# Leaving the first shift out of the normalised rows of a hybrid attention layer, and adding its product where each projection leaves its bank

## The chip, the cores and the metric

One Trainium2 chip, one of its cores. The metric is device time in microseconds (us) of one execution of the whole kernel. The engines are named PE (TensorE), ACT (ScalarE), DVE (VectorE), POOL (GpSimd) and SP (SyncE, which here only issues DMAs).

## The reference, cut to what matters

One layer of an encoder runs over two request groups with the same weights: 1024 prompt tokens, and 32 sample tokens that see a cache of 512. D_MODEL is 1024. Each group has one vector `c`, from which the modulation vectors come. The part that the change touches is the way into the one combined projection:

```python
ada = jax.nn.silu(c) @ w_ada + b_ada                 # w_ada: 1024 x 6144
sh1, sc1, gt1, sh2, sc2, gt2 = [a[:, None, :] for a in jnp.split(ada, 6, axis=-1)]
h = rms_norm(x, g_pre_mix) * (1 + sc1) + sh1
p = h @ w_in                                         # w_in: 1024 x 4256
q_lat, c_kv, k_r, q_b, k_b, v_b, g_a, g_b = jnp.split(p, IN_SPLITS, axis=-1)
```

The eight parts of `p` feed two attention branches: latent attention (`q_lat`, `c_kv`, `k_r`) and stick-breaking attention (`q_b`, `k_b`, `v_b`, eight heads of 64), which are merged by the sigmoids of `g_a` and `g_b`. An output projection and a convolutional feed-forward part (1024 to 5632, and 2816 back to 1024) follow. All is float32. Outputs are the two groups' rows and the new cache entries, among them the K and V rows of the stick-breaking branch.

## The kernel before, in words

Everything is kept transposed: features on the 128 partitions, tokens along the free axis. The 1024 prompt tokens and the 32 sample tokens stand side by side, T = 1056 columns. A float32 product is made of three products of shorter numbers: each operand is split into a high part (`hi`, on ACT) and the remainder (`lo`, on DVE), and `mm3` multiplies high by high, high by low and low by high into one PSUM bank.

`stage_h` makes the normalised, modulated rows. Eight tiles of x (`load`) are fetched and scaled by their root mean square. `ada_half` makes shift and scale for one half of the 1024 features: eight DMAs of 512 KB of `w_ada`, 32 small products, two transposes (line 239), one addition of the bias. `norm_T` transposes x on PE (line 263), applies scale and shift with one ACT instruction per 512 columns (line 265), and DVE splits the result into `Hht` and `Hlt` (lines 268 and 269), eight tiles of 128 features each. The order written down is: first half of the modulation, rows of tokens 0 to 511 and 512 to 1023 for those features, then two weight tiles, then the second half of the modulation and the rows for it.

`w_in_tile` fetches 128 columns of `w_in` and splits them; there are 34 such tiles. `mtile` makes the product of one weight tile with the rows in three blocks of NB = 352 columns (`BLK`), 8 x 3 = 24 PE instructions a block, each block in one PSUM bank. There are eight banks: two tagged `mm`, two `tr`, three `s`, one `pv`.

`stage_sb` runs over four pairs of heads. `sb_pair` makes Q (split as it leaves the bank, scaled by 0.125), K and V, puts K and V into natural order by transposes for the cache outputs (`to_natural`), and sweeps the blocks of queries (`attend`: scores at lines 452 to 456, `sb_weights` on ACT and DVE, transposes, values). After each pair `gates` makes four of the 16 gate tiles; DVE copies each block out of its bank (line 633) and a DMA stores it. Between them `ada_step` makes the other four modulation vectors. `stage_lat` makes the rotated key, the two kv-latent tiles and the three query-latent tiles; a query-latent block is read from its bank by ACT twice (high part, line 60; square, line 809) and by DVE once (line 810). Merge, MLA attention, feed-forward and output stages follow; they don't use the rows `Hht` and `Hlt`.

The order of instructions on each engine isn't that of the source: a planner orders them when the program is built, by its own costs and the data they wait for, so that gate products stand between the steps of the attention. Each engine then works its list in order. Buffers rotate in the order of the source: a pool gives a tag so many buffers, and a new tile waits for the last reader of the tile that had its buffer.

Of the kernel before, what the change touches and what calls it, by code (L numbers as in the profile page):

```python
# [39 lines left out]
class K:  # L40
# [183 lines left out]
    def ada_half(self, hf, wp, tp):  # L224

        nc, a = self.nc, self.a
        acc = self.tl(tp, [P, 256], F32, f"ada{hf}")
        ps = self.bank("s")
        for k in range(KT):
            w = self.tl(wp, [P, 2, 512], F32, "wr")  # L230
            nc.sync.dma_start(w, a["w_ada"][0, k * P : (k + 1) * P].rearrange("p (v h n) -> p v h n", v=6, h=2)[:, 0:2, hf])
            for j in range(4):
                c = (j % 2) * 256
                nc.tensor.matmul(ps[32 * j : 32 * j + 32, :256], self.cT[:, k], w[:, j // 2, c : c + 256],
                                 start=k == 0, stop=k == KT - 1)
        nc.vector.tensor_copy(acc, ps[:, :256])
        tr = self.bank("s")
        for c in range(2):
            nc.tensor.transpose(tr[:, c * P : c * P + P], acc[:, c * P : c * P + P], self.idt)
        for c in range(2):  # L240
            k = slice(4 * hf + c, 4 * hf + 4, 2)
            nc.vector.tensor_tensor(self.adaT[:, 0:2, k],
                                    tr[:, c * P : c * P + P].rearrange("p (v j r) -> p v j r", v=2, j=2)[:, :, :, 0:2],
                                    self.bT[:, :, k].unsqueeze(3).broadcast_to([P, 2, 2, 2]), ALU.add)
        self.gain(self.g1, 1, 0, 4 * hf, 4)


    def norm_T(self, t0, xs, g, sv, tp, k0=0, k1=KT):


        nc = self.nc
        if t0 < 8:
            n = len(xs) * P
            m = 512 // n
            c = slice(t0 * P, t0 * P + n)
            for k in range(k0, k1, m):
                tr = self.bank("tr")
                f = self.tl(tp, [P, 512], F32, "hf").rearrange("p (k c) -> p k c", k=m)
                for e in range(m):
                    kc = slice((k + e) * P, (k + e) * P + P)  # L260
                    for j, x in enumerate(xs):
                        o = e * n + j * P
                        nc.tensor.transpose(tr[:, o : o + P], x[:, kc], self.idt)
                for e in range(m):
                    nc.scalar.activation(f[:, e], tr[:, e * n : e * n + n], AF.Identity,
                                         bias=self.adaT[:, sv, k + e, 0:1], scale=g[:, k + e, 0:1])
                h, l = self.Hht[:, k : k + m, c], self.Hlt[:, k : k + m, c]
                nc.vector.tensor_copy(h, f)
                nc.vector.tensor_tensor(l, f, h.bitcast(F32), ALU.subtract)
        else:  # L270
            tr = self.bank("tr")
            for c in range(2):
                nc.tensor.transpose(tr[:, c * P : c * P + P], xs[0][:, c * P : c * P + P], self.idt)
            f = self.tl(tp, [P, 512], F32, "hf")[:, :256].rearrange("p (k t) -> p k t", t=TS)
            for k in range(k0, k1):
                j, c = k // 2, k % 2
                nc.scalar.activation(f[:, k], tr[:, c * P + 32 * j : c * P + 32 * j + 32],
                                     AF.Identity, bias=self.adaT[:, sv, k, 1:2], scale=g[:, k, 1:2])
            f, h, l = (x[:, k0:k1] for x in (f, self.Hht[:, :, TP:T], self.Hlt[:, :, TP:T]))
            nc.vector.tensor_copy(h, f)  # L280
            self.lo(l, f, h)
# [22 lines left out]
    def new_H(self):  # L304
        self.Hp = self.tc.alloc_tile_pool(name=self.nm("H"), bufs=1, side="right", reuse_waits="tile")
        self.Hht = self.Hp.tile([P, KT, T], F32R, name=self.nm("hh"))
        self.Hlt = self.Hp.tile([P, KT, T], F32R, name=self.nm("hl"))
        self.Hh = [self.Hht[:, k] for k in range(KT)]
        self.Hl = [self.Hlt[:, k] for k in range(KT)]

    def stage_h(self):
# [3 lines left out]
        with self.tc.tile_pool(name="st_h", bufs=2, reuse_waits="tile") as tp, self.tc.tile_pool(name="wada", bufs=8, reuse_waits="tile") as wp:  # L315
# [9 lines left out]
            def norm(t, hf):  # L325
                self.norm_T(t, xts[t : t + 4] if t < 8 else [xs], self.g1, 0, tp, 4 * hf, 4 * hf + 4)
# [8 lines left out]
            for t in range(4, 8):  # L335
                load(t)
            norm(4, 0)
            xs = self.tl(tp, [P, 256], F32, "xs")
            self.quarters(xs, a["x_sample"][0])
            w = [self.w_in_tile(672), self.w_in_tile(672 + 512)]  # L340
            self.in_w = w
            self.ada_half(1, wp, tp)
            nc.vector.tensor_scalar(xs, xs, self.rstd_s(xs, tp), None, ALU.mult)
            norm(0, 1)
            norm(8, 0)
            norm(4, 1)
            norm(8, 1)
# [14 lines left out]
    def w_in_tile(self, c0):  # L362
# [3 lines left out]
        h, l = self.wsplit(raw)  # L366
        v = lambda t: t.rearrange("p (k c) -> p k c", k=8)
        return v(h), v(l)
# [13 lines left out]
    def sb_pair(self, p):  # L382
# [5 lines left out]
        wh, wl = self.w_in_tile(q0)  # L388
        for c0, n, ps in self.mtile(wh, wl, self.Hh, self.Hl, self.BLK, KT):
            m = min(n, TP - c0)  # L390
            c = slice(c0, c0 + m)
            self.hi(Qe[0:64, c], ps[0:64, :m], 0.125)
            self.hi(Qo[64:128, c], ps[64:128, :m], 0.125)
            st = nc.vector.scalar_tensor_tensor
            st(Qe[64:128, c], ps[0:64, :m], 0.125, Qe[0:64, c].bitcast(F32), ALU.mult, ALU.subtract)
            st(Qo[0:64, c], ps[64:128, :m], 0.125, Qo[64:128, c].bitcast(F32), ALU.mult, ALU.subtract)
            if m < n:
                nc.scalar.mul(self.qsb[:, p], ps[:, m:n], 0.125)
# [5 lines left out]
        wh, wl = self.w_in_tile(k0)  # L404
        for c0, n, ps in self.mtile(wh, wl, self.Hh, self.Hl, self.BLK, KT, "mm" if p else "s"):
            nc.scalar.copy(kf[:, c0 : c0 + n], ps[:, :n])
# [27 lines left out]
        wh, wl = self.w_in_tile(v0)  # L434
        for c0, n, ps in self.mtile(wh, wl, self.Hh, self.Hl, self.BLK, KT):
            nc.scalar.copy(vf[:, c0 : c0 + n], ps[:, :n])  # L436
# [188 lines left out]
    def gates(self, ms):  # L625
        nc = self.nc
        for m in ms:
            wh, wl = self.w_in_tile(2208 + m * P)
            if self.ada_todo:
                self.ada_step(2, self.W, self.At)  # L630
            for c0, n, ps in self.mtile(wh, wl, self.Hh, self.Hl, self.BLK, KT):
                g = self.tl(self.At, [P, 512], F32, "nat")
                nc.vector.tensor_copy(g[:, :n], ps[:, :n])
                nc.gpsimd.dma_start(self.gd[m, :, c0 : c0 + n], g[:, :n])

    def att_pools(self):
# [13 lines left out]
        nc.sync.dma_start(self.qt, self.a["k_ropeq"])  # L650
# [58 lines left out]
    def stage_lat(self):  # L709
# [15 lines left out]
        def latent(m0, n, pool, tag):  # L725
            f = []
            for m in range(m0, m0 + n):
                x = self.tl(pool, [P, T], F32, tag)
                f.append(x)
                wh, wl = self.w_in_tile(m * P)  # L730
                for c0, n_, ps in self.mtile(wh, wl, self.Hh, self.Hl, self.BLK, KT, "mm s s"):
                    nc.scalar.copy(x[:, c0 : c0 + n_], ps[:, :n_])
# [33 lines left out]
        for c0, n, ps in self.mtile(hv, lv, self.Hh, self.Hl, self.BLK, KT, "mm s s"):  # L766
# [4 lines left out]
            nc.vector.tensor_tensor(ta[64:128, :n], ps[0:64, :n], ct[0:64, :n], ALU.mult)  # L771
            nc.vector.tensor_tensor(tb[64:128, :n], ps[64:128, :n], ct[64:128, :n], ALU.mult)
# [28 lines left out]
        sq = self.tl(self.At, [P, BIG], F32, "big")  # L801
        for m in range(3):
            wh, wl = self.w_in_tile(m * P)
            g = self.gvT[:, 16 + m : 17 + m]
            for c0, n, ps in self.mtile(wh, wl, self.Hh, self.Hl, self.BLK, KT, "mm s s"):
                c, ps = slice(c0, c0 + n), ps[:, :n]
                self.hi(self.QLh[m][:, c], ps, g)
                d = self.tl(self.At, [P, 512], F32, "nat")[:, :n] if m else sq[:, c]
                nc.scalar.activation(d, ps, AF.Square)
                nc.vector.scalar_tensor_tensor(self.QLl[m][:, c], ps, g, self.QLh[m][:, c].bitcast(F32), ALU.mult, ALU.subtract)  # L810
# [973 lines left out]
```

## Time and profile before

| | |
|---|---|
| median of 3 runs | 1828.43 us (1828.35 to 1831.26) |
| the profiled execution | 1828.67 us |
| its span, first to last instruction | 1826.9 us |
| granted PE clock, mean | 0.987 |
| DMA over the span | 124 GB/s |

In the views below, a row of busy time by stretch reads: stretch in us, its length, then for PE, PE's weight loads (PEld), DVE, ACT and POOL the busy us and the number of instructions, the granted clock, the share of the 16 DMA engines' time, and GB/s. A row for one tile or line shows the engines that touch it. A row of the timeline reads: start in us, duration in us, engine, line, operation, output and inputs with partitions and elements, count, and in brackets the idle time before it and what ended it. A row of the waits reads: who waited for whom, us in total, times, longest. Matmuls are pipelined, so their starts tell the pace and their durations overlap.

### The profile page before, as it was taken

How to read it: one execution, taken by the hardware profiler on the slowest of the kernel's cores; microseconds unless marked ns; L12 is line 12 of the kernel's file. 1: busy time of each engine (PE TensorE's matmuls, PEld its weight loads, DVE VectorE, ACT ScalarE, POOL GpSimd, SP SyncE). 2: the span in 40 equal slices, each digit the busy share in tenths (PEclk: the TensorE clock that was granted, in tenths of full speed). 3: DMA queues.
4: the chain of work that ended last, by engine and by line, in shares of the span. 5: the costliest groups of instructions: out<-in, count | busy, mean ns of one | idle time of the engine just before them, and what ended most of it. 6: DMA issues, size and time to landing. Idle time of an engine off the chain costs nothing. (4 is left out here: it accounts for less than half of the span.)

```text
span 1826.9 us, 30116 instructions
## 1 busy us (share of the span) xinstructions
PE 1745.1 (96%) x11610; PEld 1552.6 (85%) x11610; DVE 1263.8 (69%) x2099; ACT 1001.0 (55%) x1913; POOL 257.4 (14%) x522
## 2 busy tenths in 40 slices
PE   6999999999899999999989998999999999999997
PEld 3888878878778988888878877999999999977876
DVE  4677377486378457777666677987877777788546
ACT  4565366564366458788687256544544444544432
POOL 2112111111111101111110022221211111110001
PEclk8999999999999999999999999999999999999999
DMA  9223333233232112222238352244233333497536
GB/s 339 74 88 111 94 99 87 76 99 101 93 97 82 54 57 72 80 71 77 64 123 269 124 179 108 67 152 140 93 122 132 101 111 132 166 338 257 164 90 220
DMA packets 182319, 228.61 MB, mean 125 GB/s; under 512 B 13509, under 2 KB 130208, under 8 KB 182176
## 3 DMA queue, kind: packets, MB, share of 16 engines
q1 hardware_dynamic: 166752, 182.93, 31.7%
q0 software_dynamic: 15424, 43.76, 6.8%
q8 instruction: 91, 1.49, 0.3%
q14 instruction: 52, 0.43, 0.1%
HBM read 174.86 MB, written 51.79 MB: 124 GB/s over the span
## 5 line engine op out<-in xcount | busy, mean ns | idle before, releaser
L60 ACT ACTIVATE wh<-wr 128x1024 fp32r<-128x1024 f32 (+6 forms) x187 | 150.7, 816 | 264.8 <-PE s L1248 86.6
L63 DVE TENSOR_TENSOR wl<-wr,wh 128x1024 fp32r<-128x1024 f32 (+6 forms) x187 | 169.5, 913 | 135.7 <-ACT wh L60 133.9
L67 PE MATMUL mm<-hh,wh 128*128 128x352 f32 x696 | 229.9, 330 | 0.6 <-ACT big L436 0.6
L69 PE MATMUL mm<-hh,wl 128*128 128x352 f32 x696 | 228.9, 329 | 0.0
L68 PE MATMUL mm<-hl,wh 128*128 128x352 f32 x696 | 228.0, 328 | 0.0
L67 PEld LDWEIGHTS mm<-hh,wh 128*128 128x128 f32 x696 | 132.1, 190 | 6.5 <-DVE ada L201 2.5
L69 PEld LDWEIGHTS mm<-hh,wl 128*128 128x128 f32 x696 | 132.1, 190 | 1.1 <-issue 0.8
L68 PEld LDWEIGHTS mm<-hl,wh 128*128 128x128 f32 x696 | 131.9, 189 | 1.3 <-issue 0.4
L530 PE MATMUL tr<-c,A 128*128 128x128 f32 x576 | 93.8, 277 | 5.4 <-ACT A L478 4.2
L1249 PE MATMUL s<-T,wl 128*128 128x256 f32 (+1 forms) x328 | 93.4, 285 | 0.0
L1248 PE MATMUL s<-T,wh 128*128 128x256 f32 (+1 forms) x328 | 93.3, 285 | 0.0
L1247 PE MATMUL s<-T,wh 128*128 128x256 f32 (+1 forms) x328 | 93.3, 284 | 0.0
L474 DVE TENSOR_TENSOR_SCAN A<-A 128x128 f32<-128x128 f32 (+8 forms) x66 | 87.8, 1343 | 0.3
L1385 DVE SCALAR_TENSOR_TENSOR u<-u,c,u 128x1058 f32<-128x1058 f32 x68 | 86.9, 1315 | 1.2
L530 PEld LDWEIGHTS tr<-c,A 128*128 128x128 f32 x576 | 66.6, 140 | 15.9 <-ACT A L478 10.2
L63 DVE TENSOR_TENSOR PTl<-tr,PTh 128x512 fp32r<-128x512 f32 x96 | 62.9, 683 | 24.1 <-ACT PTh L60 23.5
L1247 PE MATMUL tr<-T,wh 128*128 128x272 f32 (+1 forms) x272 | 77.9, 286 | 0.0
L1249 PE MATMUL tr<-T,wl 128*128 128x272 f32 (+1 forms) x272 | 77.4, 285 | 0.0
L1248 PE MATMUL tr<-T,wh 128*128 128x272 f32 (+1 forms) x272 | 77.3, 284 | 0.0
L478 ACT ACTIVATE A<-A 128x128 f32<-128x128 f32 (+8 forms) x66 | 44.3, 680 | 60.0 <-DVE A L477 59.7
L63 DVE TENSOR_TENSOR wl<-S,wh 128x1024 fp32r<-128x1024 f32 x40 | 48.9, 1222 | 37.5 <-ACT wh L60 37.5
L1247 PE MATMUL mm<-T,wh 128*128 128x256 f32 (+1 forms) x256 | 73.2, 286 | 0.0
(598 smaller groups left out, 5571.8 us busy)
## 6 DMA issues: line engine op xcount, KB each, us to landing
wr<-in_w_ada_dram SPq DMA_DIRECT2D x48, 512.0 KB, 5.0
wr<-in_w_up_dram SPq DMA_DIRECT2D x44, 512.0 KB, 4.1
dr<-in_w_down_dram SPq DMA_DIRECT2D x43, 512.0 KB, 5.8
wr<-gdn SPq DMA_DIRECT2D x34, 512.0 KB, 4.5
wr<-in_w_in_dram SPq DMA_DIRECT2D x33, 512.0 KB, 4.0
gdn<-u POOLq DMA_DIRECT2D x23, 512.0 KB, 4.5
gd<-nat POOLq DMA_DIRECT2D x48, 176.0 KB, 2.5
t<-gd SPq DMA_DIRECT2D x16, 528.0 KB, 4.7
```

Source lines behind the costliest of these rows:

```text
L60: self.nc.scalar.activation(out, in_, AF.Identity, scale=scale)
L63: return self.nc.vector.tensor_tensor(out, full, hi.bitcast(F32), ALU.subtract)
L67: m(ps, lh, rh, start=start, stop=False)
L68: m(ps, lh, rl, start=False, stop=False)
L69: m(ps, ll, rh, start=False, stop=stop)
L474: nc.vector.tensor_tensor_scan(r, r, r, 0.0, ALU.add, ALU.bypass)
L478: nc.scalar.activation(A[:, :w], A[:, :w], AF.Exp)
L530: nc.tensor.transpose(tr[:, (2 * s + q) * P : (2 * s + q + 1) * P], at[q][:, b * P : b * P + P], self.idt)
L1247: m(ps[:, :n], w[0][:, k], x[0][:, k, c], start=first and k == 0, stop=False, skip_group_check=True)
L1248: m(ps[:, :n], w[0][:, k], x[1][:, k, c], start=False, stop=False, skip_group_check=True)
L1249: m(ps[:, :n], w[1][:, k], x[0][:, k, c], start=False, stop=k == 3, skip_group_check=True)
L1385: nc.vector.scalar_tensor_tensor(y, u[:, w : w + YW], self.cvT[:, w, cc : cc + 1], y, ALU.mult, ALU.add)
```

## The change

`ada_half` becomes `ada_first`, which makes one whole vector: the scale first, the shift last. The rows of the prompt get the scale alone; the transposed bank is split directly, high part by ACT, remainder by DVE. `Hht` and `Hlt` get two more columns (T to T + 2) that both hold the prompt's shift. The sample's rows still get a shift: the difference of the two groups' shifts, so that the prompt's shift is what is missing from all columns.

For each weight tile the block with columns 704 to 1057 (`SHB`, 354 columns) is now made first; its column 352 is the product of the shift with the weight tile. It is copied out (`bias`), and every block is added to it as it leaves its bank: by ACT's `plus`, in the gates by DVE. Only in the first head pair the blocks 0 and 1 of Q and K come first, in four banks, and the third blocks after them. The 0.125 of Q goes into its weight tile. In the query latents each sum is first written to a tile `nat`, from which high part, remainder and square are made. The table `qt` for the queries is loaded in `stage_lat`, no more in `att_pools`.

```diff
-    def ada_half(self, hf, wp, tp):
+    def ada_first(self, v, wp, tp):
...
-            nc.sync.dma_start(w, a["w_ada"][0, k * P : (k + 1) * P].rearrange("p (v h n) -> p v h n", v=6, h=2)[:, 0:2, hf])
+            nc.sync.dma_start(w, a["w_ada"][0, k * P : (k + 1) * P, v * D : v * D + D])
...
     norm_T:
-                    nc.scalar.activation(f[:, e], tr[:, e * n : e * n + n], AF.Identity,
-                                         bias=self.adaT[:, sv, k + e, 0:1], scale=g[:, k + e, 0:1])
-                nc.vector.tensor_copy(h, f)
-                nc.vector.tensor_tensor(l, f, h.bitcast(F32), ALU.subtract)
+                self.hi(h, tr, gk)
+                nc.vector.scalar_tensor_tensor(l, tr, gk, h.bitcast(F32), ALU.mult, ALU.subtract)
...
     stage_h, after load(0) to load(3):
-            self.ada_half(0, wp, tp)
-            norm(0, 0)
+            self.ada_first(1, wp, tp)
+            self.gain(self.g1, 1, 0)
+            w = [self.w_in_tile(672, 0.125)]
...
             for t in range(4, 8):
                 load(t)
-            norm(4, 0)
+            self.norm_T(0, xts[:4], tp, ("tr", "tr", "s", "s", "s"))
+            w.append(self.w_in_tile(672 + 512))
...
-            self.ada_half(1, wp, tp)
+            self.norm_T(4, xts[4:], tp, ("tr",))
...
+            self.ada_first(0, wp, tp)
+            h, l = (x[:, :, T : T + 2] for x in (self.Hht, self.Hlt))
+            sh = self.adaT[:, 0, :, 0:1]
+            nc.vector.tensor_copy(h, sh.broadcast_to([P, KT, 2]))
+            self.lo(l, sh.broadcast_to([P, KT, 2]), h)
+            d = self.tl(tp, [P, KT], F32, "shd")
+            nc.vector.tensor_tensor(d, self.adaT[:, 0, :, 1], self.adaT[:, 0, :, 0], ALU.subtract)
+            self.norm_T(8, [xs], tp, shift=d)
...
+    SHB = (2 * NB, NB + 2)
+
+    def h_tile(self, w, tags="mm", copy=None):
+        tags = tags.split()
+        for i, blk in enumerate((self.SHB, *self.BLK[:2])):
+            c0, n, ps = next(self.mtile(*w, self.Hh, self.Hl, (blk,), KT, tags[i % len(tags)]))
+            if i == 0:
+                b = self.bias(ps, copy)
+            yield c0, ps[:, :NB], b
+
+    def bias(self, ps, copy=None):
+        b = self.tl(self.sm, [P, 1], F32, "bb")
+        (copy or self.nc.scalar.copy)(b, ps[:, NB : NB + 1])
+        return b
+
+    def plus(self, out, ps, b):
+        self.nc.scalar.activation(out, ps, AF.Identity, bias=b)
...
     sb_pair:
+        wq, wk = self.w_in_tile(q0, 0.125), self.w_in_tile(k0)
+        if p == 0:
+            first = [next(self.mtile(*w, self.Hh, self.Hl, (blk,), KT, g))[2] for w, blk, g in (
+                (wq, self.BLK[0], "mm"), (wk, self.BLK[0], "s"), (wq, self.BLK[1], "mm"), (wk, self.BLK[1], "s"))]
+            for w, f, g in ((wq, q_out, "s"), (wk, lambda c0, ps, b: self.plus(kf[:, c0 : c0 + NB], ps, b), "tr")):
+                c0, n, ps = next(self.mtile(*w, self.Hh, self.Hl, (self.SHB,), KT, g))
+                b = self.bias(ps)
+                for x in (0, 1):
+                    f(x * NB, first[2 * x + (w is wk)][:, :NB], b)
+                f(c0, ps[:, :NB], b)
...
     gates:
-                nc.vector.tensor_copy(g[:, :n], ps[:, :n])
+                nc.vector.tensor_scalar(g, ps, b, None, ALU.add)
...
     stage_lat, query latents:
-                self.hi(self.QLh[m][:, c], ps, g)
-                d = self.tl(self.At, [P, 512], F32, "nat")[:, :n] if m else sq[:, c]
-                nc.scalar.activation(d, ps, AF.Square)
+                f = self.tl(self.At, [P, 512], F32, "nat")[:, :n]
+                self.plus(f, ps, b)
+                self.hi(self.QLh[m][:, c], f, g)
...
+                d = f if m else sq[:, c]
+                nc.scalar.activation(d, f, AF.Square)
```

More of the change, by code (lines that the diff above doesn't have):

```diff
@@ new lines, in ada_first, with norm_T @@
+        nc.vector.tensor_tensor(self.adaT[:, v].rearrange("p (j c) e -> p c j e", c=2),
+                                tr[:, :256].rearrange("p (c j r) -> p c j r", c=2, j=4)[:, :, :, 0:2], b, ALU.add)
+    def norm_T(self, t0, xs, tp, tags=None, shift=None):
+        nc, g = self.nc, self.g1
+        if t0 < 8:
+            c = slice(t0 * P, t0 * P + 512)
+            for k in range(KT):
+                tr = self.bank(tags[k % len(tags)])
+                for j, x in enumerate(xs):
+                    nc.tensor.transpose(tr[:, j * P : j * P + P], x[:, k * P : k * P + P], self.idt)
+                h, l, gk = self.Hht[:, k, c], self.Hlt[:, k, c], g[:, k, 0:1]
+                self.hi(h, tr, gk)
+                nc.vector.scalar_tensor_tensor(l, tr, gk, h.bitcast(F32), ALU.mult, ALU.subtract)
```

135 lines of the change are left out of this document (56 added, 79 removed).

## The prediction

> **What bounds the kernel now.** I read the page first, then the busy time by stretch, then the opening engine by engine.
>
> ```profile
> span 1826.9 us, 30116 instructions
> PE 1745.1 (96%) x11610; PEld 1552.6 (85%) x11610; DVE 1263.8 (69%) x2099; ACT 1001.0 (55%) x1913; POOL 257.4 (14%) x522
> PE   6999999999899999999989998999999999999997
> PEclk8999999999999999999999999999999999999999
> ```
>
> TensorE (PE) is busy nearly everywhere; only the first of the 40 slices (45.7 us) shows 6 and a clock of 8. So time is won where PE waits or does its work late, and that is the opening, which is also where the change is. The next rows cut the opening at 47.49 us, where the second half of the modulation vectors reaches PE, and at 83.74 us, where the Q, K and V products of the first head pair end. First all engines, then the tile `mm` alone, then the transposes of line 263 alone.
>
> ```profile
> 22.00:47.49 25.49, 19.55 (x132) 12.09 (x124) 14.91 (x29) 12.45 (x20) 4.68 (x10) 0.67 1.03 338
> 47.49:83.74 36.25, 36.25 (x231) 34.49 (x232) 21.40 (x41) 18.54 (x35) 3.08 (x4) 1.00 0.17 49
> 22.00:47.49 25.49, 7.10 (x24) 4.98 (x24) 0.00 (x0) 0.00 (x0) 0.67 1.03 338
> 22.00:47.49 25.49, 8.31 (x32) 5.33 (x32) 0.67 1.03 338
> 47.49:83.74 36.25, 3.83 (x24) 2.52 (x24) 1.00 0.17 49
> ```
>
> Up to 47.49 us PE has done 24 of the 216 products (3 weight tiles x 3 blocks x 24), and 40 of the 64 transposes (8 ran before 22 us). From then on it is busy 36.25 of 36.25 us. The first stretch moves 338 GB/s at a DMA share of 1.03: that is the modulation weights arriving. What PE does meanwhile, and how fast:
>
> ```profile
> 33.12 0.64 PE L67 MATMUL mm<-hh,wh 128*128 128x352 f32 x1
> 38.44 0.49 PE L67 MATMUL mm<-hh,wh 128*128 128x352 f32 x1
> 38.73 0.48 PE L68 MATMUL mm<-hl,wh 128*128 128x352 f32 x1
> ...
> 40.94 0.32 PE L67 MATMUL mm<-hh,wh 128*128 128x352 f32 x1
> 41.10 0.32 PE L68 MATMUL mm<-hl,wh 128*128 128x352 f32 x1
> ...
> 45.01 1.93 PE L234 MATMUL s<-wr,cT 128*32 128x256 f32 x32
> 47.49 0.44 PE L239 MATMUL s<-c,ada 128*128 128x128 f32 x2 [0.55 <-DVE ada L236]
> ...
> 49.36 0.66 PE L263 MATMUL tr<-c,x 128*128 128x128 f32 x4
> 49.82 0.43 PE L67 MATMUL mm<-hh,wh 128*128 128x352 f32 x1
> ...
> 83.74 1.25 PE L379 MATMUL tr<-c,big 128*128 128x128 f32 x8
> 84.75 0.36 PE L452 MATMUL s<-KH,Q 128*128 128x256 f32 x1
> ```
>
> Products start at 33.12 us; starts lie 0.29 us apart while the clock is low and 0.16 us once it is up. The first scores start at 84.75 us.
>
> **The change, part by part.**
>
> *More products before the shift is known.* Before, `ada_half` delivers scale and shift for half the rows, so only half of each sum can run before 47.49 us. After, the scale comes whole, and four blocks (Q and K weights, token blocks 0 and 1, 96 products) need no shift. The new program's PE order puts 53 products and all 64 transposes ahead of the two transposes that finish the shift (the old L239). Had those stood at 47.49 us again, there would be left 216 - 53 = 163 products instead of 192 and no transposes instead of 24: 29 x 0.16 = 4.7 us, and six groups of four transposes at up to 0.46 us (49.36 to 49.82), 2.5 us, so 7.2 us; with the sample rows' transposes and the switches between groups that fall away, some 8 us. It is the first term.
>
> *When that point comes.* ScalarE (ACT) paces it:
>
> ```profile
> 23.11 1.06 ACT L99 ACTIVATE jk<-x 128x1024 f32<-128x1024 f32 x1 [10.99 <-DMA x<-in_x_prompt_dram]
> 24.44 1.45 ACT L265 ACTIVATE hf<-tr,c,c 128x512 f32<-128x512 f32 x2 [0.18 <-DVE c L220]
> ...
> 29.51 1.05 ACT L99 ACTIVATE jk<-x 128x1024 f32<-128x1024 f32 x1
> 30.46 0.19 ACT L99 ACTIVATION_READ_ACCUMULATOR jk<-x 128x1 f32 x1
> 30.55 1.05 ACT L60 ACTIVATE wh<-wr 128x1024 fp32r<-128x1024 f32 x1
> ```
>
> The first weight tile is queued ahead of x rows 4 to 7 now, so it is split at about 23.2 us and those rows come one 512 KB transfer later. From 24.4 us ACT has 16 evictions at 1.45 / 2 = 0.73 us (11.6), four sums of squares at 1.04 (4.2), the second split (1.05) and the sample sum (0.5): 17.4 us, to 41.8. The last eight evictions share two `tr` banks, each held through transposes, ACT's read and now VectorE's (DVE's) read too: 0.66 + 0.73 + 0.76 and some 0.25 of hand-overs, about 2.4 us for two evictions instead of 2 x 0.73, so 4 x 0.95 = 3.8 us more; the rows are whole at about 45 us and the shift is finished at about 46.3, against 47.49. That is a gain of 1.2 us, between 3.5 (ACT alone sets it) and -2.5 (PE at the low clock). Opening: 8 + 1.2 = 9.2 us, range 5.5 to 11.5.
>
> *DVE in the opening* loses a copy and reads a bank instead:
>
> ```profile
> L268 DVE CAST hh<-hf x16: 405/420/427, 25.9 to 59.9; 128x512 fp32r<-128x512 f32 x16
> L269 DVE TENSOR_TENSOR hl<-hf,hh x16: 619/691/693, 26.3 to 60.9; 128x512 fp32r<-128x512 f32 x16
> ```
>
> 16 x 0.42 = 6.7 us of DVE work go; 16 remainders at 0.69 to 0.76 stay. DVE is off the path there (14.91 of 25.49 us), so I take nothing. The shift columns, differences and sample rows add about 5 us of small steps after the shift; 43 products (6.9 us) hide them. Without that cover they would cost up to 5 us.
>
> *Two more columns* in one block of each of 34 tiles: 34 x 24 x 2 columns at 0.16 / 352 us = 0.7 us on PE, on the path.
>
> *Adding the shift as a bank is emptied.*
>
> ```profile
> L398 ACT ACTIVATE qsb<-mm x4: 197/197/198, 69.7 to 460.2; 128x32 f32<-128x32 f32 x4
> L60 ACT ACTIVATE lat<-s,c 128x352 fp32r<-128x352 f32 x6 | 3.3, 544 | 0.2 <-PE s L69 0.2
> L809 ACT ACTIVATE nat<-s 128x352 f32<-128x352 f32 x4 | 1.8, 452 | 0.0
> L633 DVE COPY nat<-mm 128x352 f32<-128x352 f32 x48 | 24.7, 514 | 21.1 <-PE mm L69 20.9
> L478 ACT ACTIVATE A<-A 128x1024 f32<-128x1024 f32 x8 | 8.4, 1052 | 13.5 <-DVE A L477 13.5
> ...
> PE s L452 <- DVE A L477: 12.8, 21, 1.8
> PE s L607 <- ACT A L599: 5.0, 1, 5.0
> ```
>
> 33 column copies on ACT (about 0.2 us) and one on DVE, 0.09 us more for evictions with a bias pointer (544 against 452 ns), nine additions of 0.55 us in the query latents: some 18 us more for an engine that is 55% busy, nearly all beside PE. What is new is a wait: the 16 gate tiles were emptied by DVE alone and now wait for ACT's copy, behind which DVE's score steps are queued, and behind those PE's `s` banks (the 12.8 us row). Bounds: -2 us (the planner has regrouped the queues, and a reorder can help as well) to 6 us (0.2 us in each of 28 tiles of the attention stage). A second `mm` bank covers 24 x 0.16 = 3.8 us, far above 0.2, so I take 1.5.
>
> *The query latents.* Tiles `nat`, two buffers, now hold the sum for the first latent too; it went straight from its bank before.
>
> ```profile
> 642.79 0.46 ACT L809 ACTIVATE nat<-mm 128x352 f32<-128x352 f32 x1
> 646.48 0.58 ACT L799 COPY lat<-tr 64x512 f32<-64x512 f32 x1 [3.23 <-PE tr L798]
> ```
>
> Those buffers come free around these times, so the first latent's banks, done before 640 us until now, wait. Five banks hold 5 x 3.8 = 19 us of products, so 0 to 4 us; I take 0.5. The table moved for the queries comes into the queue at nearly its old place: nothing. From the first MLA head pair on all orders are the old ones, so what is won by then is kept.
>
> **Sum.** 1828.67 us, the profiled execution's own time (span 1826.9; 0.24 above the median of 1828.43, less than a run varies): -9.2 + 0.7 + 1.5 + 0.5 = -6.5, so **1822.2 us**.
>
> **The rivals.**
>
> *The clock stays low.*
>
> ```profile
> 20.00:30.00 10.00, 5.34 (x30) 2.83 (x30) 5.08 (x12) 6.50 (x11) 3.01 (x6) 0.60 1.08 351
> 30.00:40.00 10.00, 8.14 (x38) 5.40 (x40) 8.89 (x15) 5.94 (x10) 0.93 (x3) 0.55 1.05 379
> 40.00:50.00 10.00, 9.45 (x94) 6.37 (x86) 1.97 (x8) 1.45 (x2) 0.74 (x2) 1.00 0.70 214
> ```
>
> From 20 to 40 us the granted clock is 0.60 and 0.55 though PE is half to 8 tenths busy, and the early products fall into just that stretch. If it stays low until the shift is there, K's 24 products cost 24 x 0.13 = 3.1 us more and the 32 later transposes about 0.1 each: 6.3 us, which leaves a gain of 2.9 and a total of 1828.5. Against it: steady products brought it to 1.00 in the next row. The Trainium skill (TensorE: Matmul & The Clock Gate, Part 1) says that half rate is the default, that one sustained busy window of about 3.4 us releases it and an idle one takes it back; by that rule ACT-paced gaps are the danger before 37 us and the dense stretch after it runs at full clock, which the three rows bear out, so the sum stays. Chance 0.13.
>
> *The new wait decides (slower).* DVE stands for ACT's column copy in each gate tile; if an exponential of 1.05 us is ahead of it, that is 1.25 us x 16 = 20 us of DVE, and if the scores are late by it, PE idles as in the 12.8 us row. Full price 1828.7 - 9.2 + 0.7 + 20 = 1840 us; it decides once PE's new idle time passes about 8.5 us. For it: DVE and ACT alternate in every score step. Against: products fill PE's gaps, and no row has PE waiting long for a gate's bank. Chance 0.08.
>
> *The shift is waited for all the same (the change does not do what it says).* PE works in order, and 43 of the 96 products stand behind the shift. Its weights are still last in the DMA queue; every us past 46.3 costs one, and at 55 the gain is gone: 1828. Against: the DMA share falls to 0.70 in 40 to 50 us, so most have landed by the early 40s. Chance 0.05.
>
> **How the numbers follow.** Forecast 0.74, rivals 0.13, 0.08, 0.05. A measurement of this kernel tells 0.2% (3.7 us) from no change: faster is below 1824.8, slower above 1832.1. The forecast and 0.02 of the first rival are faster (0.76), the rest of it and the third within (0.16), the second slower (0.08). Range: 11.5 won with costs near 0 gives 1816; at the top it takes in the first and third rivals, 1829.
>
> **What would show it.** Right: Q products from 25 to 26 us, the shift's last transposes at 45 to 47.5, first scores near 75 instead of 84.75, and that lead of 9 us down to 6 or 7 at the first MLA products. Wrong: the scores' start under 5 us earlier (opening), a lead that shrinks by over 4 us between there and the latents with DVE idle behind ACT's column copies (the wait), or PE waiting in the latents for `nat` (buffers).

## The result, and the profile after

| | before | after |
|---|---|---|
| median of nine runs each | 1828.35 us (1825.46 to 1831.26) | 1834.50 us (1830.97 to 1838.27) |
| ratio | | 1.003 (95% interval 1.002 to 1.004) |
| the profiled execution | 1828.67 us | 1830.97 us |
| its span and granted clock | 1826.9 us, 0.987 | 1829.2 us, 0.992 |

By the ratio the change made the kernel 5.5 us slower (6.2 by the two medians), where the forecast had it 6.5 us faster. The profiled execution after is the fastest of its nine, so the two traces differ by less than the medians do.

The head of the page after:

```profile
span 1829.2 us, 30109 instructions
PE 1745.8 (95%) x11608; PEld 1558.5 (85%) x11608; DVE 1264.4 (69%) x2082; ACT 1013.8 (55%) x1955; POOL 251.9 (14%) x522
```

PE's total is the old one (1745.8 against 1745.1 us): the change moves PE's work and hardly alters it. The busy time by stretch, after, cut where the shift's two transposes reach PE (52.23 us) and where the first scores start (81.10 us), and the row that stood for the low clock before:

```profile
22.00:52.23 30.23, 25.76 (x172) 17.55 (x169) 18.00 (x28) 16.45 (x28) 4.41 (x10) 0.89 0.84 289
52.23:81.10 28.87, 28.14 (x177) 27.60 (x176) 13.29 (x24) 14.03 (x30) 2.88 (x4) 1.00 0.18 56
30.00:40.00 10.00, 8.55 (x58) 5.92 (x56) 7.58 (x11) 6.75 (x13) 1.53 (x3) 0.97 1.02 395
```

The timeline of PE after, at the three places that the prediction named:

```profile
24.95 0.66 PE L67 MATMUL mm<-hh,wh 128*128 128x352 f32 x1 [1.79 <-ACT hh L60]
...
52.23 0.38 PE L238 MATMUL pv<-c,ada 128*128 128x128 f32 x2
...
81.11 0.36 PE L480 MATMUL s<-KH,Q 128*128 128x256 f32 x1
```

The products start at 24.95 us as forecast, but the shift's transposes stand at 52.23 us instead of 46.3, and the first scores at 81.11 us instead of 75. What PE did just before, first as a stretch, then by line between the same two moments (the groups' busy us and mean ns):

```profile
37.00:52.23 15.23, 15.23 (x116) 9.38 (x115) 6.11 (x11) 4.01 (x6) 0.74 (x2) 1.00 0.64 202
```

```profile
L233 PE MATMUL pv<-wr,cT 128*32 128x256 f32 x56 | 6.3, 391 | 0.0
L254 PE MATMUL tr<-c,x 128*128 128x128 f32 x24 | 3.5, 277 | 0.0
```

From 37 us to the shift's transposes PE is busy 15.23 of 15.23 us at full clock, 6.3 of them in the modulation's own products; ACT, which was to set the pace, is busy 4.01 and stands waiting for PE's transposes. ACT's waits in the same stretch:

```profile
ACT hh L60 <- PE tr L254: 6.5, 5, 2.5
```

The further way, as the start of the same PE instruction in two profiled runs, other kernel minus before, in us (negative is earlier). The moments are V's first transpose of pair 0, K's first transpose of pairs 1, 2 and 3 (line 379 before), the first ones product of the kv latents (line 681), and the first instructions of line 909 in the MLA stage and of line 1215 behind it. Each figure is one execution; two runs with the same opening differ by up to 1.7 at the first mark.

| at (us in before) | 83.7 | 202.4 | 338.5 | 468.4 | 622.1 | 691.7 | 1072.4 |
|---|---|---|---|---|---|---|---|
| after | -2.8 | -0.8 | +0.1 | +3.7 | -0.2 | +2.9 | +3.5 |
| opening alone | -2.6 | -2.3 | -1.5 | 0.0 | +0.4 | +0.1 | +1.6 |
| evictions alone | +0.1 | +2.8 | +2.5 | +5.0 | +3.5 | +5.9 | +6.4 |
| own buffers | -1.8 | +0.9 | +0.6 | +3.2 | +0.5 | +3.5 | +4.6 |
| gates' column by DVE | -2.5 | +0.9 | +9.4 | +12.2 | +17.4 | +19.9 | +19.6 |
| no column | -3.0 | +1.4 | +0.8 | +4.9 | +1.0 | +3.7 | +4.4 |
| no column, old order | -2.4 | -1.2 | +2.1 | +4.2 | +7.9 | +11.8 | +13.6 |
| V in the old order | -2.6 | -2.0 | +0.9 | +1.8 | +6.4 | +9.2 | +11.5 |
| late | +6.8 | +7.2 | +6.3 | +7.5 | +7.6 | +7.5 | +7.3 |
| no shift in the opening | -10.9 | -10.5 | -11.6 | -10.1 | -10.0 | -5.8 | -3.5 |

So the opening is won and pair 0 gives some 2 us back. Pair 2 (338 to 468 us) costs 3.6, pair 3 (468 to 622) returns 3.9, and the latents (622 to 692) cost 3. In pair 2 the granted clock falls for a while, from 355 to 365 us, first before, then after:

```profile
355.00:365.00 10.00, 8.33 (x52) 7.26 (x53) 9.58 (x20) 9.55 (x22) 1.37 (x3) 1.00 0.48 142
355.00:365.00 10.00, 7.38 (x30) 5.98 (x27) 8.75 (x16) 6.92 (x17) 1.05 (x3) 0.66 0.69 213
```

In pair 3 a stall of the kernel before is gone, the 5.0 us of line 607 among its waits:

```profile
492.40 0.71 PE L607 MATMUL s<-A,QZ 128*64 128x272 f32 x1 [4.97 <-ACT A L599]
```

Every kernel here that makes V in the old order has this stall (3.6 to 5.0 us), and none that makes V in the new order. So the evictions' loss is what is left after this gain. PE's waits after, from 80 to 600 us and then from 615 to 695:

```profile
PE s L480 <- DVE A L505: 13.6, 22, 1.9
PE tr L558 <- ACT A L506: 5.7, 10, 1.2
PE mm L199 <- DVE nat L661: 1.9, 2, 1.0
PE mm L67 <- DVE ada L201: 1.7, 4, 0.6
```

```profile
PE mm L708 <- DVE big L842: 2.8, 3, 1.8
PE s L67 <- ACT nat L370: 1.1, 1, 1.1
```

The waits for DVE's score steps are nearly the old ones (12.8 us in 21). New are small waits for banks behind DVE's queue, and in the latents a wait for the sum of squares (line 842) and one for a bank that ACT empties into `nat` (line 370).

### The profile page after: what moved, and what is told of

Read it like the earlier page. It is cut to its first block, busy times and chain, and to the rows that moved or that the text cites. A ratio compares the mean times of both kernels' runs of the same rounds, so it can differ in the third digit from the quotient of the medians.

```text
span 1829.2 us, 30109 instructions
## 1 busy us (share of the span) xinstructions
PE 1745.8 (95%) x11608; PEld 1558.5 (85%) x11608; DVE 1264.4 (69%) x2082; ACT 1013.8 (55%) x1955; POOL 251.9 (14%) x522
## 5 line engine op out<-in xcount | busy, mean ns | idle before, releaser
L63 DVE TENSOR_TENSOR wl<-wr,wh 128x512 fp32r<-128x512 f32 (+4 forms) x183 | 164.9, 907 | 133.2 <-ACT wh L60 125.2
L67 PE MATMUL mm<-hh,wh 128*128 128x352 f32 (+1 forms) x688 | 229.3, 333 | 4.2 <-ACT hh L60 1.8
L68 PE MATMUL mm<-hl,wh 128*128 128x352 f32 (+1 forms) x688 | 228.0, 331 | 1.4 <-DVE hl L257 1.4
L69 PE MATMUL mm<-hh,wl 128*128 128x352 f32 (+1 forms) x688 | 226.1, 329 | 0.0
L67 PEld LDWEIGHTS mm<-hh,wh 128*128 128x128 f32 x688 | 131.0, 190 | 11.5 <-DVE ada L201 4.4
L558 PEld LDWEIGHTS tr<-c,A 128*128 128x128 f32 x576 | 67.5, 141 | 15.4 <-ACT A L506 10.5
```

Of the source, the lines that this page charges most:

```text
L63: return self.nc.vector.tensor_tensor(out, full, hi.bitcast(F32), ALU.subtract)
L67: m(ps, lh, rh, start=start, stop=False)
L68: m(ps, lh, rl, start=False, stop=False)
L69: m(ps, ll, rh, start=False, stop=stop)
L558: nc.tensor.transpose(tr[:, (2 * s + q) * P : (2 * s + q + 1) * P], at[q][:, b * P : b * P + P], self.idt)
```

## The experiments

Two theories stood at the start. **A**: the evictions lose, later, what the opening wins. **B**: the opening's own lead is lost on the way. Each median stands beside runs of the kernel before on the same chip, whose median was 1828.4 to 1830.1 us from call to call; ratios are therefore what is compared.

**The two halves of the change apart.** `opening_alone` keeps the changed `stage_h` and pair 0's Q and K, and takes all else from the kernel before; its PE order from the end of the opening is the old one. `evictions_alone` is the reverse:

```diff
 opening_alone: all tiles but pair 0's Q and K
-        for c0, ps, b in self.h_tile(self.w_in_tile(v0)):
-            self.plus(vf[:, c0 : c0 + NB], ps, b)
+        wh, wl = self.w_in_tile(v0)
+        for c0, n, ps in self.mtile(wh, wl, self.Hh, self.Hl, self.BLK, KT):
+            nc.scalar.copy(vf[:, c0 : c0 + n], ps[:, :n])
 ... the same for the other tiles
 evictions_alone: the old stage_h, pair 0's Q and K as before, and
...
+            nc.gpsimd.memset(x[:, :, T : T + 2].bitcast(F32), 0.0)     # x in Hht, Hlt
```

> The changed opening, with pair 0's Q and K and their added shift, before a kernel that is otherwise the old one: every other tile is emptied as before, without the shift, which is therefore left out of those outputs. Theory A (the loss is paid later, by the evictions): the first scores start at about 81 us as in the changed kernel, against 84.75, and nothing gives it back, so the run is 2.5 to 4 us below the kernel before, about 1825. Theory B (the opening itself costs: the early lead is eaten in the attention stage because the queues that follow are planned from another start): the lead of 3.6 us is gone by 350 us and the run is within 1.5 us of before or above it. The forecast's own term, 9.2 us, would give 1819.

> The old opening, with the shift in the rows as before and pair 0's Q and K as before; the two extra columns are zero, and from pair 0's V on all 32 other tiles go by the changed path (block 2 first, column copy, eviction with a bias). Theory A: this is where the loss is, some 3 us in the attention stage and 3.5 to 4 us in the latents, so 6 to 8 us above before, about 1835. Theory B: 0 to 2 us above before. The forecast's terms (0.7 + 1.5 + 0.5) would give 2.7 us above.

Measured: the opening alone 1828.14 us, 0.9996 (0.9986 to 1.0007); the evictions alone 1834.34 us, 1.0031 (1.0019 to 1.0043), 5.7 us above before. The evictions carry the whole loss, as theory A has it. But the opening's 2.6 us hardly arrive either: the ratio's interval just reaches them, and in the trace the lead is gone by 468 us, with the same instructions in the same order. So B holds in part. One place where it went, in the busy time by stretch, first before, then the opening alone:

```profile
350.00:360.00 10.00, 8.16 (x64) 6.45 (x64) 7.19 (x16) 8.05 (x21) 2.37 (x4) 1.00 0.54 161
```

```profile
350.00:360.00 10.00, 8.16 (x56) 6.75 (x55) 7.88 (x17) 8.28 (x21) 2.36 (x4) 0.83 0.54 161
```

and PE's timeline there, in the same two kernels:

```profile
356.66 0.47 PE L452 MATMUL s<-KH,Q 128*128 128x512 f32 x1 [1.84 <-DVE A L477]
```

```profile
355.29 0.47 PE L492 MATMUL s<-KH,Q 128*128 128x512 f32 x1 [1.84 <-DVE A L517]
```

It is the same stall of 1.84 us. After it the clock stayed at 1.00 in one run and was halved for a while in the other, and the lead fell from 1.4 us to 0.4 between 351 and 386 us.

**Does a shift of the opening reach the end?** `late` computes pair 0's K blocks 0 and 1 once more in the kernel before, 48 products that nobody reads; `opening_no_shift` is the opening alone with a shift of zero:

```diff
 late, in sb_pair for p == 0
+            for _ in self.mtile(wh, wl, self.Hh, self.Hl, self.BLK[:2], KT, "s"):
+                pass
 opening_no_shift, in stage_h
-            self.ada_first(0, wp, tp)
+            nc.vector.memset(self.adaT[:, 0], 0.0)
```

> The kernel before, with pair 0's K blocks 0 and 1 computed once more ahead (48 products of 0.16 us into banks that nobody reads, 7.7 us of PE in the opening). All later instructions keep their order. If time won or lost in the opening goes through to the end, this is 7 to 8 us above before, 1836. If the attention stage absorbs such a shift (the engines catch up in its waits), it is 3 us or less above. The run with the opening alone brought 0.3 us where its first scores were 2.6 us early, so this tells whether a lead is absorbed or was within the scatter of the runs.

> The run with the opening alone, and its shift is set to zero without computing it: the second modulation vector's products (64 rows, 6.95 us busy) and its weights' transfers are left out, so nothing waits for them. If PE's own work bounds the opening from 37 us on (busy 15.23 of 15.23 us up to the shift's transposes), the first scores come earlier by about that work, 6 to 8 us, from 82.1 to 74 to 76. If PE had stood waiting for the shift, they come 10 us or more earlier. The end should follow by 5 to 7 us, to about 1822.

Measured: late 1834.24 us, 1.0027 (1.0014 to 1.0040), so 4.9 us (2.6 to 7.3), where 7.7 were forecast from the products' pace and 6.8 stood at the first mark; it was 7.3 us late at 1072 us and its profiled execution ended 4.7 us late. Without the shift 1824.15 us, 0.9959 (0.9943 to 0.9974), so 7.5 us (4.8 to 10.4) of the 10.9 at the first scores, which started here (a stretch, and a row of the timeline):

```profile
37.00:50.00 13.00, 13.00 (x90) 12.42 (x89) 7.49 (x12) 6.04 (x14) 0.74 (x2) 1.00 0.33 94
```

```profile
73.86 0.36 PE L492 MATMUL s<-KH,Q 128*128 128x256 f32 x1
```

That is 8.3 us before the opening alone (82.12), about the 6.95 us of products left out and their switches, with PE again busy without a gap. PE's own work bounds the opening; it did not stand waiting for the shift. This run leaves out the shift's weight transfers too, so it is the rows without a gap, beside the 8.3 us, that show it. On the way this kernel lost 4.2 us between 622 and 692 us, most of it to a wait that the old timing hides (0.5 us before):

```profile
PE tr L837 <- DMA nat<-in_cache_mla_krope_dram: 2.9, 1, 2.9
```

So a shift of the opening goes through in good part. That some of `late`'s is lost is not shown, since its interval takes in the 6.8 us; the interval of the run without a shift ends just under the 10.9 us, and the DMA wait is one place where it loses.

**The query latents' buffers.** `own_buf` is the changed kernel with

```diff
-                f = self.tl(self.At, [P, 512], F32, "nat")[:, :n]
+                f = self.tl(self.At, [P, TP], F32, "A")[:, :n] if m else sq[:, c]
```

> The changed kernel, but the query latents' sum goes into the sum-of-squares row itself for the first latent and into a buffer of tile A for the other two, no longer into nat. If the two nat buffers hold the banks back, the wait of PE for a bank before the ones products disappears and the run is 2 to 4 us below the changed kernel, about 1831. If the loss in the latents is instead the length of ACT's own queue there (27.4 to 34.0 us busy out of 50 between 640 and 690 us), it stays within 1 us.

Measured 1831.37 us, 1.0016 (1.0005 to 1.0027): 2.6 us under the changed kernel by the ratios, though the intervals overlap. Its waits of PE from 615 to 695 us:

```profile
PE s L67 <- ACT wh L60: 2.5, 1, 2.5
PE mm L708 <- DVE big L842: 0.2, 1, 0.2
```

The wait before the ones products went from 2.8 to 0.2 us and the one for `nat` is gone; in their place PE waits 2.5 us for ACT to split a weight tile (0.6 before), with ACT as busy there as in the changed kernel. So the latents took as long as ever in this execution. From the first ones product to the first MLA scores, the changed kernel and then this one:

```profile
621.80:694.60 72.80, 68.11 (x429) 63.11 (x428) 44.81 (x86) 50.98 (x108) 3.40 (x5) 1.00 0.21 60
622.60:695.20 72.60, 69.58 (x428) 64.20 (x427) 44.32 (x86) 50.04 (x108) 3.41 (x5) 0.98 0.20 59
```

PE stands 1.7 us less and is busy 1.5 us longer at a lower clock. Where the 2.6 us of the ratios come from, the trace doesn't show.

**The column copy and the order of blocks.** Three kernels on the wait that the prediction priced at 1.5 us:

```diff
 gates_dve
-            for c0, ps, b in self.h_tile(w):
+            for c0, ps, b in self.h_tile(w, copy=nc.vector.tensor_copy):
 no_column, in h_tile
-                b = self.bias(ps, copy)
+                b = self.nob                      # a constant column of zeros
 no_column_old_order, in h_tile, beside that
-        for i, blk in enumerate((self.SHB, *self.BLK[:2])):
...
+        for c0, n, ps in self.mtile(*w, self.Hh, self.Hl, self.BLK, KT, " ".join(tags)):
```

> The changed kernel, with the column of the 16 gate tiles copied by DVE instead of ACT. If DVE standing for ACT's copy is what costs the attention stage, PE's waits for score steps fall back by about 1 us, the stage gives back up to 3 us, and the run is about 1831.5. If the loss there is the added work itself or the new order of blocks, the run stays within 1 us of the changed kernel.

> The changed kernel, but a constant zero column takes the place of the copied one in all tiles after pair 0's Q and K (the shift is left out of their outputs): block order, the two extra columns and the evictions with a bias stay, the copy and the wait for it go. If the copy and its wait are what the 32 tiles cost in the attention stage, the 2.7 us lost between the end of pair 0's V products and pair 1's keys fall below 1 us and the run is 2 to 3 us below the changed kernel, about 1832. If the block order or the longer evictions cost it, the run stays within 1 us of the changed kernel.

> As the run with the constant zero column, and the blocks of those tiles go in the old order (0, 1, 2) at the old width. What is left of the change then is the opening, the bias evictions and the query latents' sum. If the order is what costs (V's first four transposes need blocks 0 and 1, which come last in the new order), this is 2 to 3 us below the run with the zero column alone. If copy and wait cost it, the two runs agree within 1 us. The query latents should still lose their 2 to 3 us in both.

Measured: 1853.21 us (1.0129, 1.0116 to 1.0143), 1832.10 us (1.0018, 1.0010 to 1.0027) and 1842.07 us (1.0073, 1.0058 to 1.0088). Taking the ACT copy out of the gates' way cost 18 us (0.0099), and the kernel with least in it, no copy and the old order, was slower than the one with the new order. No theory had foreseen either. The copy itself and its wait are worth some 2.4 us by the medians (1834.50 against 1832.10, intervals overlapping), and pair 0's loss stays without them (-3.0 to +1.4 us).

One step in pair 1, and the like in pair 3, is where much of this is lost: of the 22 us from the first mark to the last, pairs 1 and 3 hold 13.7 with the gates' column on DVE, and 7.0 of 16 without column in the old order, which also has the stall of line 607 again (3.6 us). The rest was not traced. The timeline of DVE and PE with the gates' column on DVE, then the same without column in the old order:

```profile
266.62 0.58 DVE L661 TENSOR_SCALAR nat<-mm,bb 128x352 f32<-128x352 f32 x1 [2.31 <-PE mm L69]
267.12 0.88 DVE L500 SCALAR_TENSOR_TENSOR A<-s,A 128x512 f32<-128x512 f32 x2
267.92 2.60 DVE L502 TENSOR_TENSOR_SCAN A<-A 128x1024 f32<-128x1024 f32 x2
...
271.15 0.58 PE L480 MATMUL s<-KH,Q 128*128 128x256 f32 x1 [3.25 <-DVE A L505]
```

```profile
264.62 0.58 DVE L661 TENSOR_SCALAR nat<-mm,c 128x352 f32<-128x352 f32 x1 [2.30 <-PE mm L69]
...
269.15 0.58 PE L480 MATMUL s<-KH,Q 128*128 128x256 f32 x1 [3.25 <-DVE A L505]
```

DVE stands 2.3 us for a gate tile's products with a score step queued behind, and the next scores then wait 3.25 us with no product left to fill them. What follows, busy time from 268 to 278 us in these two and then in the changed kernel:

```profile
268.00:278.00 10.00, 6.85 (x28) 5.98 (x28) 6.83 (x10) 4.50 (x9) 0.04 (x1) 0.66 0.54 175
```

```profile
268.00:278.00 10.00, 8.85 (x45) 7.96 (x45) 6.52 (x13) 5.98 (x12) 0.00 (x0) 0.66 0.42 147
```

```profile
268.00:278.00 10.00, 9.26 (x62) 8.47 (x61) 8.12 (x13) 6.40 (x15) 0.57 (x1) 1.00 0.31 100
```

In 10 us PE issues 28 and 45 instructions instead of 62: the stall, and then half clock. The changed kernel has no such stall here; the planner had put the gate's eviction elsewhere.

**V alone in the old order.** `v_old_order` changes only the V tiles:

```diff
-        for c0, ps, b in self.h_tile(self.w_in_tile(v0)):
-            self.plus(vf[:, c0 : c0 + NB], ps, b)
+        wh, wl = self.w_in_tile(v0)
+        for c0, n, ps in self.mtile(wh, wl, self.Hh, self.Hl, self.BLK, KT):
+            nc.scalar.copy(vf[:, c0 : c0 + n], ps[:, :n])
```

> The changed kernel, with the four V tiles emptied as before, blocks 0, 1, 2 at the old width and without the shift (left out of V). If the order of V's blocks is what costs pair 0, the lead against before no longer shrinks by 1 to 3 us between pair 0's K transposes (71 us) and pair 1's (202 us), and the run is 2 to 3 us below the changed kernel. If the whole plan of the stage decides (where the gates' products stand among the score steps), the run may go either way, by as much as the run in the old order (13.6 us above before), and the waits for DVE's score steps show which.

Measured 1838.40 us, 1.0054 (1.0039 to 1.0069). Both expectations came true in part: pair 0 now loses 0.6 us (-2.6 to -2.0) where the changed kernel lost 2.0, and the whole is slower. The stall of 3.25 us is there in both places, and the 5.0 us stall of line 607 (in the kernel before) has come back. The stall of 3.25 us:

```profile
267.76 0.39 PE L481 MATMUL s<-KH,Q 128*128 128x256 f32 x1 [3.25 <-DVE A L506]
...
544.20 0.39 PE L481 MATMUL s<-KH,Q 128*128 128x256 f32 x1 [3.25 <-DVE A L506]
```

That V's block order costs pair 0 some 2 us is borne out by the two kernels with the old order and by the opening alone; which of V's transposes or evictions does it was not tried. The new V tiles also take the stall of line 607 out of pair 3: they are all that differs between this kernel and the changed one.

**A version to beat both, and its control.** In `own_buf_gates_act` ACT empties the gate tiles too, so nobody stands for another engine's column; `squares_dve` adds DVE for the query latents' squares; `before_gates_act` is the kernel before with that one idea of ACT for the gates, and `opening_gates_act` puts the opening alone on it:

```diff
 own_buf_gates_act
-                nc.vector.tensor_scalar(g, ps, b, None, ALU.add)
+                self.plus(g, ps, b)
 squares_dve, beside that
-                nc.scalar.activation(d, f, AF.Square)
+                nc.vector.tensor_tensor(d, f, f, ALU.mult)
 before_gates_act; opening_gates_act has the same beside opening_alone
-                nc.vector.tensor_copy(g[:, :n], ps[:, :n])
+                nc.scalar.copy(g[:, :n], ps[:, :n])
```

> The changed kernel with the query latents' sum out of nat, and the 16 gate tiles emptied by ACT with a bias instead of by DVE: copy and eviction now stand in one queue, DVE loses 48 evictions of 0.57 us, ACT gains 48 of 0.55 us. If DVE standing for ACT's column is what the attention stage pays, PE's waits for DVE's score steps (13.6 us from 80 to 600 us) fall by 2 to 4 us and the run is 2 to 4 us below that with its own buffers (1831.4), so at or under before. If ACT's queue is the limit there, exponentials come late and it is 3 us or more above it.

> The run with its own buffers and the gates by ACT, and the query latents' squares (9 of 0.55 us) computed by DVE instead of ACT. If ACT's longer queue is what is left of the loss in the latents (PE waited 2.5 us there for ACT's split of a weight tile), that wait goes and the run is 2 to 3 us lower, about 1825.5, under before. If not, it stays within 1 us of 1827.7, or another wait takes its place.

> The kernel before, untouched but for one word: its 16 gate tiles are copied out of their banks by ACT instead of DVE. This is the control for the run that equals before (own buffers, gates by ACT). If moving the gates off DVE is itself worth 2 us or more, because PE's waits for DVE's score steps (12.8 us) fall, this run is at or under 1826.5 and the equality owes nothing to the change's opening. If it is within 1 us of before, the gates on ACT only mend what the changed evictions broke.

> The opening alone (the shift left out of all other tiles), on the kernel whose gate tiles are copied by ACT instead of DVE (1826.7, before 1830.1 beside it). Orders are the same after the opening. If the opening's lead of 2.6 us goes through, this run is 1.5 to 3 us below that kernel, at a ratio to before of 0.9960 to 0.9968. If a lead of this size is lost again on the way (the first run with the opening alone ended 0.3 us under before), the ratio stays at 0.9975.

| | median | ratio to before |
|---|---|---|
| own_buf_gates_act | 1827.73 us | 0.9995 (0.9987 to 1.0004) |
| squares_dve | 1827.03 us | 0.9986 (0.9975 to 0.9997) |
| before_gates_act | 1826.72 us | 0.9975 (0.9965 to 0.9986) |
| opening_gates_act | 1823.11 us | 0.9970 (0.9960 to 0.9980) |

The first brings the change back to before. The waits for DVE's score steps did not fall as expected (13.7 us against 13.6); the small ones for banks did. The squares' wait for the split went (2.5 us to two rows of under 0.6), with no gain in time that the intervals show; in the traces the latents cost 1.2 us there (622 to 692, against before), where they cost 3.2 with the squares on ACT and 2.4 to 3.9 in every other kernel with the changed latents. So the latents' loss hangs on ACT's work there, for the most part. The control then takes the credit away: on the kernel before, ACT for the gates is worth 4.6 us (2.6 to 6.4) by itself, and its ratio is the lowest of the kernels here that leave nothing out. PE's waits for the score steps from 80 to 600 us, first with own buffers and gates by ACT, then in the control:

```profile
PE s L480 <- DVE A L505: 13.7, 20, 1.8
```

```profile
PE s L452 <- DVE A L477: 12.1, 20, 1.8
PE tr L530 <- ACT A L478: 3.5, 5, 0.9
```

These waits move little (12.8 and 4.2 before), so what makes the control faster is spread over many steps and was not settled. The opening on top of it changes the ratio by 0.0005, 0.9 us, less than the intervals can tell.

## Why the prediction was wrong, point by point

**The opening, 9.2 us: the step that failed is "when that point comes".** The first term was right: from the shift's transposes to the first scores, 37.26 us before (84.75 - 47.49) became 28.88 (81.11 - 52.23), 8.4 us against 8. The second, 1.2 us for the shift at 46.3, was -4.7: 52.23 against 47.49. I had taken ACT as the pacer and never added up PE's own work ahead of that point. The 53 products and 64 transposes that come before the shift by the new order, and the 6.3 us of modulation products that I left out altogether, fill PE without a gap from 37 us on, and ACT waits 6.5 us for PE's transposes there, the reverse of what I had. The trace after gives the sum: PE is busy 25.76 us from 22 us to that point, so at this clock it stands at 47.8 at the earliest, with no gap at all, and not at 46.3. The rows of before could only have warned: from 22 us on they have 25.49 - 19.55 = 5.94 us of idle PE, and work brought forward can win no more than idle time and what a low clock costs (some 19.55 x 0.33 = 6.5 us, an estimate from the clock of 0.67). So 9.2 asked for all the idle time and half of that besides. What was won from cut to cut is 83.74 - 81.10 = 2.64 us: PE's idle time fell by 0.74, to 5.20 (30.23 - 25.76 and 28.87 - 28.14), and its busy time by 1.9 (19.55 + 36.25 to 25.76 + 28.14) as the clock rose (0.67 to 0.89 in the first stretch). My lower end, 5.5, had PE slow by its clock, but not full.

**"What is won by then is kept": only in part.** The opening alone ended 0.7 us below before, on the second base 0.9, of 2.6 at the first scores; `late` passed on 4.9 of 6.8 to 7.7, the run without a shift 7.5 of 10.9. Each has an interval of about 2 to 3 us to a side, and `late` may have lost nothing of the 6.8 us at its first mark, so how much is lost is not known well; that it is lost to stalls that the clock answers differently, and to a DMA wait that becomes visible, is shown at one place each.

**Columns, wait and buffers, 0.7 + 1.5 + 0.5 = 2.7 us: measured 5.7 (3.5 to 7.9) with the evictions alone.** The latents were the term most mis-sized: some 3 us (2.4 to 3.9 in the traces) where I took 0.5 of a range up to 4. The buffers' wait is there as foreseen, but it is not the whole mechanism: with other buffers the latents cost 3.0 all the same, and with less work for ACT 1.2. For the attention stage some 2 us remain (5.7 - 0.7 - 3) where I took 1.5, and this near hit is luck: it is what larger sums leave, V's order in pair 0 and the low clock in pair 2 against the stall that pair 3 lost. The mechanism I gave isn't seen: without the copy pair 0 loses as much, with V's old order it doesn't. My bounds for the regrouped plan, -2 to 6 us, were too narrow for what a plan can do: moving the gates' one column to another engine took the changed kernel from 1834.5 to 1853.2 us, and moving their evictions took it from 1831.4 to 1827.7.

The parts add up: -0.7 from the opening and 5.7 from the evictions make 5.0, against 5.5 measured. Of the 12 us between forecast and result, 6.6 are the opening, 1.9 what was lost of it on the way, and 3.0 the evictions. (The lower end of my range was also added wrongly: 11.5 won at no cost gives 1817, not 1816.)

**The rivals.** *The clock stays low* did not come: 0.97 from 30 to 40 us where before had 0.55. The stretch from 37 us ran at 1.00, as the forecast took it. *The new wait decides* did not happen in the changed kernel, whose score waits rose by 0.8 us. A relative of it shows in three experiments, which were slower than before by 24.8, 13.6 and 9.2 us: a score wait of 3.25 us, with DVE standing for a gate tile and score steps behind it. But there DVE stood for PE's products, not for ACT's copy, which the two slowest leave out of the gates, so it is luck that my price of 1840 lies near them. I gave it 0.08 because no row of before showed PE waiting long for a gate's bank; that row could not tell what another plan would do. *The shift is waited for* named the right quantity (every us past 46.3 costs one: 5.9 late leaves 3.3, measured 2.6) with a wrong cause: PE did not wait, it was full.

## What to carry to other kernels

Before crediting a move with the time it fills, add up the moved engine's own work to the point that matters: in a stretch the gain is at most the idle time there plus what a low clock costs. Where a planner orders the queues, an edit of evictions all along a stage is a new plan, and the plan's spread (here 18 us for one small copy on another engine) belongs in the range. Look for what the new plan won as well: here it took out a stall of 5 us. And try the repair on the old kernel too: ACT for the gates was worth as much without the change (4.6 us) as with it (3.8, from 1.0016 to 0.9995).

## What the runs showed of the hardware

The same stall of 1.84 us was followed by full clock in one run and by a mean of 0.83 over 10 us in the next, at the same instruction, 1.4 us earlier; a stall of 3.25 us was followed by 0.66 in both kernels shown, and by 0.83 with V in the old order:

```profile
268.00:278.00 10.00, 9.94 (x58) 8.76 (x58) 7.03 (x14) 7.80 (x16) 0.00 (x0) 0.83 0.29 97
```

The Trainium skill (TensorE: Matmul & The Clock Gate, Part 1) says that the activity window runs freely, about 3.4 us long, and that an idle one brings half rate. That fits, except that these stalls are shorter than a window. So a stall here cost more than its length by an amount that differed from run to run, down to nothing, and runs of one program scatter with their clock: the changed kernel's spans went from 1829.2 us at a mean clock of 0.992 to 1836.5 at 0.986.

The first product after a group of another kind took more than the usual pace: in the dense stretch from 37 us the rows of the first product after a modulation group show 0.43 us where the ones behind it show 0.32 to 0.33, and its successor starts 0.26 us later instead of 0.16 to 0.17.

```profile
40.77 0.43 PE L68 MATMUL s<-hl,wh 128*128 128x352 f32 x1
41.03 0.33 PE L69 MATMUL s<-hh,wl 128*128 128x352 f32 x1
41.20 0.33 PE L67 MATMUL s<-hh,wh 128*128 128x352 f32 x1
```
